# A two-layer decoder trunk on one core: the feed-forward's split weights in a ring of the stage's own pool, and start addresses that differ from pass to pass

## The chip, the core and the metric

The kernel runs on one core of a Trainium2 chip. Its engines work side by side: TensorE (PE) multiplies matrices, VectorE (DVE) and ScalarE (ACT) do elementwise work, GpSimd (POOL) does some of it too, SyncE (SP) issues the transfers. Operands lie in the core's on-chip memory, SBUF, which has 128 partitions; a tile takes the same range of bytes in every partition. Results of TensorE go to PSUM.

The metric is the time of one execution in microseconds of the device, as the median of several runs. Before the change it is 2267.64 us (three runs, 2267.16 to 2267.98).

## What is computed

Two decoder layers on 256 tokens of width 2048, all in float32. The first layer mixes tokens with gated linear attention (GLA), the second with stick-breaking attention; each has a feed-forward stage behind it:

```python
def swiglu(h, w_gate_up, w_down):
    gate, up = jnp.split(h @ w_gate_up, 2, axis=-1)
    return (jax.nn.silu(gate) * up) @ w_down

for layer in range(2):
    a = rmsnorm(h, attn_norm_w[layer])
    h = h + (gla_mixer(a, ...) if layer == 0 else stick_breaking(a, k_shared, v_shared, ...))
    h = h + swiglu(rmsnorm(h, ffn_norm_w[layer]), ffn_w_gate_up[layer], ffn_w_down[layer])
return rmsnorm(h, final_norm_w)
```

`w_gate_up` is 2048 x 11264 and `w_down` 5632 x 2048 in each layer.

## The kernel before

**Split products.** Every large product is made of three matmuls of type float32r: each operand is split into a rounded part and the rest, and `hi*hi`, `hi*lo` and `lo*hi` are added in PSUM. `load_w` (L111) brings weights in pieces of 128 partitions x 1024 values: SP issues the transfer into a `raw` tile (L115), ACT casts it into `hi` (L119), DVE subtracts to get `lo` (L120). `raw` has 4 buffers (pool `wraw`), `hi` and `lo` have 3 each (pool `wsp`), shared by all stages of the program.

**The product.** `gemm_tok` (L123) takes a block of 512 output columns. For each of the K tiles of 128 rows and each of the two token tiles it issues three matmuls (L137): stationary is 128 x 128 of the activations, moving is 128 x 512 of `hi` or `lo`. So each piece of weights feeds 12 matmuls, each with a stationary load of its own.

**Feed-forward.** `ffn` (L247) goes through the 11 blocks of 512 hidden columns in three passes (`PASSES`: 4, 4 and 3 blocks). A pass first makes the hidden blocks: for each, a gate product and an up product over 16 K tiles (192 matmuls), then SiLU, product, and four transposes for each token tile (L266) into `hid_h` and `hid_l`, which are the split stationary operands of the second half. Then `residual_gemm` (L232) multiplies by the pass's rows of `w_down` in four column blocks and adds to `h`. In the last column block of the last pass of layer 1, `gemm_tok_in_turn` (L142) keeps four pieces of weights in a free activation tile.

Matmuls of 512 columns by pass: gate and up 768, 768, 576; down 384, 384, 288. Both layers: 4224 + 2112 = 6336.

**Order.** Instructions of an engine run in the program's order, which a scheduler fixes when the program is built; engines wait for each other by semaphores. A pool's tiles take their place when the pool is opened, and a later pool lies where an earlier one was.

**Addresses.** The allocator starts tiles at multiples of 32 bytes. In the built program every `hi`, `lo`, `xhl` (the split activations), `hid_h` and `hid_l` begins 32 bytes past a multiple of 512, in every buffer; and all slices taken from them step by 512 bytes or a multiple. So each 512-column matmul of the feed-forward begins reading both operands at 32 modulo 512. Tiles of the GLA stage's own pool (`vhl`, `sc_ih`, `sc_il`, `sc_xh`, `sc_xl`, used at L534) begin at 352 modulo 512, which is 96 modulo 128. Those of the attention stage that L607 reads (`fh`, `tri_r`) begin at 32 modulo 512 again.

Of the kernel before, what the change touches and what calls it, by code (L numbers as in the profile page):

```python
# [9 lines left out]
F32R = mybir.dt.float32r  # L10
# [6 lines left out]
P = 128  # L17
D = 2048
S = 256
# [16 lines left out]
DFF = 5632  # L36
LEVELS = (128, 64, 32, 16, 8, 4, 2, 1)
NEG = -1.0e30
PASSES = ((0, 1, 2, 3), (4, 5, 6, 7), (8, 9, 10))


@with_exitstack
def trunk_kernel(
# [20 lines left out]
    v, a, pe, g = nc.vector, nc.scalar, nc.tensor, nc.gpsimd  # L64
# [4 lines left out]
    wsp = ctx.enter_context(tc.tile_pool(name="wsp", bufs=3))  # L69
# [38 lines left out]
        return gains[:, col[key] + k : col[key] + k + 1]  # L108


    def load_w(ap, k0, nk, c0, ncol, dst=None):  # L111
        raw = wraw.tile([P, 1024], F32, name="raw")
        hi, lo = dst or (wsp.tile([P, 1024], F32R, name="hi"), wsp.tile([P, 1024], F32R, name="lo"))
        n = nk * ncol
        nc.sync.dma_start(  # L115
            raw[:, :n].rearrange("p (k c) -> p k c", k=nk),
            ap[k0 * P : (k0 + nk) * P, c0 : c0 + ncol].rearrange("(k p) c -> p k c", p=P),
        )
        a.copy(hi[:, :n], raw[:, :n])  # L119
        v.tensor_tensor(lo[:, :n], raw[:, :n], hi.bitcast(F32)[:, :n], ALU.subtract)  # L120
        return (hi[:, :n].rearrange("p (k c) -> p k c", k=nk), lo[:, :n].rearrange("p (k c) -> p k c", k=nk))

    def gemm_tok(w_ap, kt, lhs, c0, evac, k_row0=0, before=None):  # L123

        acc = [ps_acc.tile([P, NB], F32, name="acc") for _ in range(NT)]
        k0 = 0
        while k0 < kt:
            nk = 1 if before is not None and k0 < 2 else 2
            hi, lo = load_w(w_ap, k_row0 + k0, nk, c0, NB)
            if before is not None:  # L130
                before(k0)
            for j in range(nk):
                k = k0 + j
                for t in range(NT):
                    xh, xl = lhs(k, t)
                    for n, (l, r) in enumerate(((xh, hi), (xh, lo), (xl, hi))):
                        pe.matmul(acc[t], l, r[:, j, :], start=(k == 0 and n == 0), stop=(k == kt - 1 and n == 2))  # L137
            k0 += nk
        for t in range(NT):
            evac(t, acc[t])  # L140

    def gemm_tok_in_turn(w_ap, kt, lhs, c0, evac, k_row0):  # L142

        wh, wl = (w.rearrange("p (n a) s c -> p n (a s c)", n=8)[:, i : i + 4] for w in xt_pair()[2:] for i in (0, 4))
        parts = []
        for i, k0 in enumerate(range(0, kt, 2)):
            parts.append(load_w(w_ap, k_row0 + k0, 2, c0, NB, (wh[:, i, :], wl[:, i, :]) if i < 4 else None))
        for t in range(NT):
            acc = ps_acc.tile([P, NB], F32, name="acc")
            for k in range(kt):  # L150
                xh, xl = lhs(k, t)
                hi, lo = (w[:, k % 2, :] for w in parts[k // 2])
                for n, (l, r) in enumerate(((xh, hi), (xh, lo), (xl, hi))):
                    pe.matmul(acc, l, r, start=(k == 0 and n == 0), stop=(k == kt - 1 and n == 2))  # L154
            evac(t, acc)
# [76 lines left out]
    def residual_gemm(w_ap, kt, lhs, k_row0, after=None, after_tile=None):  # L232

        for nb in range(NCB):
            def evac(t, acc, nb=nb):
                hs = h[:, t, nb * NB : (nb + 1) * NB]
                v.tensor_tensor(hs, acc, hs, ALU.add)  # L237
                if after_tile is not None:
                    after_tile(nb, t)
            if after_tile is not None and nb == NCB - 1:  # L240
                gemm_tok_in_turn(w_ap, kt, lhs, nb * NB, evac, k_row0)
            else:
                gemm_tok(w_ap, kt, lhs, nb * NB, evac, k_row0)
            if after is not None:
                after(nb)

    def ffn(layer, xh, xl, r, **after):  # L247
        w_gu, w_dn = ffn_w_gate_up[layer], ffn_w_down[layer]
        lhs = lambda k, t: (xh[:, k, t * P : (t + 1) * P], xl[:, k, t * P : (t + 1) * P])
        with tc.tile_pool(name=f"ffn{layer}", bufs=2) as fp:  # L250
            for blocks in PASSES:
                hid = []
                for b in blocks:
                    hh = fp.tile([P, 4, S], F32R, name="hid_h", bufs=4)
                    hl = fp.tile([P, 4, S], F32R, name="hid_l", bufs=4)
                    hid.append((hh, hl))
                    sg = [fp.tile([P, NB], F32, name="sg", bufs=4) for _ in range(NT)]

                    def evac_gate(t, acc, sg=sg):
                        a.activation(sg[t], acc, AF.Silu, scale=r[:, t : t + 1])  # L260

                    def evac_up(t, acc, sg=sg, hh=hh, hl=hl):
                        v.scalar_tensor_tensor(sg[t], acc, r[:, t : t + 1], sg[t], ALU.mult, ALU.mult)
                        tp = ps_tr.tile([P, 512], F32, name="tr")
                        for j in range(4):
                            pe.transpose(tp[:, j * P : (j + 1) * P], sg[t][:, j * P : (j + 1) * P], ident)  # L266
                        tv = tp.rearrange("p (j c) -> p j c", j=4)
                        ts = slice(t * P, (t + 1) * P)
                        a.copy(hh[:, :, ts], tv)  # L269
                        v.tensor_tensor(hl[:, :, ts], tv, hh.bitcast(F32)[:, :, ts], ALU.subtract)  # L270

                    gemm_tok(w_gu, KD, lhs, b * NB, evac_gate)
                    gemm_tok(w_gu, KD, lhs, DFF + b * NB, evac_up)

                def hid_lhs(k, t, hid=hid):
                    hh, hl = hid[k // 4]
                    ts = slice(t * P, (t + 1) * P)
                    return hh[:, k % 4, ts], hl[:, k % 4, ts]

                residual_gemm(w_dn, 4 * len(blocks), hid_lhs, blocks[0] * 4, **(after if blocks is PASSES[-1] else {}))  # L280


    w_in = gla_w_in[0]
# [276 lines left out]
    with tc.tile_pool(name="sb", bufs=1) as sp_:  # L560
# [12 lines left out]
        for o in (0, S, ZA, ZA + P):  # L573
            g.affine_select(pen[:, o : o + P], pen[:, o : o + P], [[1, P]], ALU.is_gt, NEG, base=0, channel_multiplier=-1)

# [90 lines left out]
def build(tc, aps):  # L666
    d = dict(zip(_INS, aps))
    d['x'] = d['x'].rearrange("b s d -> (b s) d")
    d['gla_b_gate'] = d['gla_b_gate'].rearrange("l d -> (l d)")
    d['gla_gnorm_w'] = d['gla_gnorm_w'].rearrange("l d -> (l d)")  # L670
    trunk_kernel(tc, *[d[n] for n in _INS], aps[-1].rearrange("b s d -> (b s) d"))
# [20 lines left out]
```

## Time and profile before

| | |
|---|---|
| median of three runs | 2267.64 us |
| the profiled execution's own time | 2267.96 us |
| its span, first to last instruction | 2266.1 us |
| PE busy | 2252.5 us, 10618 matmuls |
| DVE, ACT, POOL busy | 1247.4, 1047.8, 58.0 us |
| transfers | 419.55 MB, 185 GB/s |
| granted TensorE clock | 0.999 of 2.4 GHz over the span |

The profile is one execution. Matmuls overlap in it: the next begins before the one ahead has ended, and ends are modelled, so a matmul's bar is longer than the distance from one start to the next. A busy PE in this profile says that work was always under way, not that the array was at its peak; the distance between starts tells how fast it went.

### The profile page before, as it was taken

To read this page: it belongs to the slowest core of one execution; us is meant where nothing else is said; L and a number is where in the kernel's file an instruction comes from. 1 tells how busy PE (TensorE), PEld (TensorE's weight loads), DVE (VectorE), ACT (ScalarE), POOL (GpSimd) and SP (SyncE) were. 2 spreads that over 40 slices of the span, in tenths; PEclk is the share of its full clock that TensorE was granted. 3 is DMA by queue.
4 is the path that set the end of the run, shared out by engine and by line. 5 is a ranking of instruction groups with operands and counts; after the bars stand their busy time and mean duration, and the time that the engine had idled before them with its cause. 6 is when DMAs were issued, how large, how long until landed. Compare 5 with 4: busy or idle time off the path is not lost.

```text
span 2266.1 us, 27101 instructions
## 1 busy us (share of the span) xinstructions
PE 2252.5 (99%) x10618; PEld 1883.7 (83%) x10618; DVE 1247.4 (55%) x1274; ACT 1047.8 (46%) x1229; POOL 58.0 (3%) x70
## 2 busy tenths in 40 slices
PE   9999999999999999999999999999999999999998
PEld 7888888888888888888888888888888888888886
DVE  6775655554554445445654567655445444554555
ACT  6555455444434443344554446544443344434444
POOL 1100000000000000000000111000000000000000
PEclk9999999999999999999999999999999999999999
DMA  8655555666666666666566654566666666666664
GB/s 233 187 155 149 169 171 189 186 187 191 190 195 188 191 191 193 194 188 192 183 186 191 186 181 145 166 188 186 193 188 193 192 190 190 189 192 192 193 186 158
DMA packets 242782, 419.55 MB, mean 185 GB/s; under 512 B 12962, under 2 KB 64254, under 8 KB 242526
## 3 DMA queue, kind: packets, MB, share of 16 engines
q1 hardware_dynamic: 242478, 416.77, 60.5%
q8 instruction: 83, 1.36, 0.3%
q10 hardware_dynamic: 176, 1.06, 0.1%
q14 instruction: 45, 0.37, 0.0%
HBM read 415.68 MB, written 2.10 MB: 184 GB/s over the span
## 4 chain that ended last, share of the span: by engine, by line
PE 98%; DMA 1%; issue 0%; DVE 0%; ACT 0%; POOLq 0%; POOL 0%; DVEq 0%; SPq 0%; ACTq 0%
PE acc L137 82%; PE acc L169 7%; PE acc L170 4%; PE tr L266 1%; PE px L485 1%; PE tr L196 1%; PE acc L172 0%; DMA raw<-in_gla_w_in_dram 0%; PE acc L154 0%; PE px L534 0%; PE px L589 0%; PE tr L620 0%; DMA h<-in_x_dram 0%; PE px L497 0%; PE tr L621 0%
## 5 line engine op out<-in xcount | busy, mean ns | idle before, releaser
L120 DVE TENSOR_TENSOR lo<-raw,hi 128x1024 fp32r<-128x1024 f32 (+1 forms) x781 | 970.2, 1243 | 918.7 <-ACT hi L119 918.0
L119 ACT CAST hi<-raw 128x1024 fp32r<-128x1024 f32 (+1 forms) x781 | 821.5, 1052 | 1025.7 <-PE acc L137 889.8
L137 PE MATMUL acc<-hi,xhl 128*128 128x512 f32 x4096 | 1273.8, 391 | 0.6 <-ACT xhl L186 0.6
L137 PEld LDWEIGHTS acc<-hi,xhl 128*128 128x128 f32 x4096 | 768.5, 188 | 159.5 <-ACT xhl L186 1.5
L137 PE MATMUL acc<-lo,xhl 128*128 128x512 f32 x2048 | 799.6, 391 | 0.0
L137 PEld LDWEIGHTS acc<-lo,xhl 128*128 128x128 f32 x2048 | 384.8, 188 | 78.9
L137 PE MATMUL acc<-lo,hid_h 128*128 128x512 f32 x680 | 264.9, 390 | 0.0
L137 PE MATMUL acc<-hi,hid_l 128*128 128x512 f32 x680 | 264.6, 389 | 0.0
L169 PE MATMUL acc<-xhl,hi 128*128 128x512 f32 x720 | 250.6, 395 | 0.4 <-ACT hi L119 0.4
L137 PE MATMUL acc<-hi,hid_h 128*128 128x512 f32 x680 | 240.7, 390 | 0.0
L170 PE MATMUL acc<-xhl,lo 128*128 128x256 f32 x768 | 204.7, 281 | 0.0
L169 PEld LDWEIGHTS acc<-xhl,hi 128*128 128x128 f32 x720 | 132.0, 188 | 26.8 <-ACT hi L119 0.8
L170 PEld LDWEIGHTS acc<-xhl,lo 128*128 128x128 f32 x768 | 144.8, 189 | 6.2
L137 PEld LDWEIGHTS acc<-hi,hid_l 128*128 128x128 f32 x680 | 127.7, 188 | 26.4
L137 PEld LDWEIGHTS acc<-hi,hid_h 128*128 128x128 f32 x680 | 127.6, 188 | 26.3
L137 PEld LDWEIGHTS acc<-lo,hid_h 128*128 128x128 f32 x680 | 127.6, 188 | 26.2
L186 ACT ACTIVATE xhl<-tr,gains 128x256 fp32r<-128x256 f32 x96 | 41.0, 470 | 30.7 <-PE tr L196 28.3
L187 DVE SCALAR_TENSOR_TENSOR xhl<-tr,gains,xhl 128x256 fp32r<-128x256 f32 x96 | 42.6, 478 | 17.5 <-ACT xhl L186 17.4
L237 DVE TENSOR_TENSOR h<-acc,h 128x512 f32<-128x512 f32 x64 | 41.2, 682 | 8.5 <-PE acc L154 5.9
L260 ACT ACTIVATE sg<-acc,n_r 128x512 f32<-128x512 f32 x44 | 30.0, 690 | 20.8 <-PE acc L137 20.8
L269 ACT CAST hid_h<-tr 128x512 fp32r<-128x512 f32 x44 | 23.6, 589 | 31.4 <-PE tr L266 31.4
L270 DVE TENSOR_TENSOR hid_l<-tr,hid_h 128x512 fp32r<-128x512 f32 x44 | 28.3, 686 | 17.3 <-ACT hid_h L269 17.3
(177 smaller groups left out, 723.4 us busy)
## 6 DMA issues: line engine op xcount, KB each, us to landing
raw<-in_ffn_w_gate_up_dram SPq DMA_DIRECT2D x352, 512.0 KB, 3.8
raw<-in_ffn_w_down_dram SPq DMA_DIRECT2D x176, 512.0 KB, 3.7
raw<-in_gla_w_in_dram SPq DMA_DIRECT2D x97, 512.0 KB, 3.8
raw<-in_sb_w_kv_dram SPq DMA_DIRECT2D x64, 512.0 KB, 3.9
raw<-in_gla_w_out_dram SPq DMA_DIRECT2D x32, 512.0 KB, 3.7
raw<-in_sb_w_q_dram SPq DMA_DIRECT2D x32, 512.0 KB, 3.6
raw<-in_sb_w_out_dram SPq DMA_DIRECT2D x32, 512.0 KB, 3.8
h<-in_x_dram SPq DMA_DIRECT2D x8, 256.0 KB, 6.4
```

The source lines that it names most:

```text
L119: a.copy(hi[:, :n], raw[:, :n])
L120: v.tensor_tensor(lo[:, :n], raw[:, :n], hi.bitcast(F32)[:, :n], ALU.subtract)
L137: pe.matmul(acc[t], l, r[:, j, :], start=(k == 0 and n == 0), stop=(k == kt - 1 and n == 2))
L169: pe.matmul(acc[c], hi[:, j, cs], both, start=first, stop=False)
L170: pe.matmul(acc[c][:, :S], lo[:, j, cs], xhl[:, k0 + j, 0, :], start=False, stop=False)
L186: a.mul(dst_h, src, scale)
L187: v.scalar_tensor_tensor(dst_l, src, scale, dst_h.bitcast(F32), ALU.mult, ALU.subtract)
L196: pe.transpose(tp[:, o : o + P], src(t)[:, j * P : (j + 1) * P], ident)
L237: v.tensor_tensor(hs, acc, hs, ALU.add)
L260: a.activation(sg[t], acc, AF.Silu, scale=r[:, t : t + 1])
L269: a.copy(hh[:, :, ts], tv)
L270: v.tensor_tensor(hl[:, :, ts], tv, hh.bitcast(F32)[:, :, ts], ALU.subtract)
```

## The change

The feed-forward no longer uses the shared ring for its split weights. While `ffn` runs, `load_w` takes them from the stage's pool, as `fhi` and `flo`, three buffers each. These tiles, and `hid_h` and `hid_l`, are 64 values longer than what is used of them, and the part in use begins at an offset that the table `PLACES` gives for each pass: one for the weights of the gate and up products, one for those of the down product, one for the hidden tiles. The arithmetic, the transfers, the matmuls and their number stay.

```diff
+PAD = 64
+
+PLACES = (((4, 8, 8), (8, 24, 24), (16, 56, 56)), ((24, 0, 4), (32, 0, 32), (48, 0, 2)))
 PASSES = ((0, 1, 2, 3), (4, 5, 6, 7), (8, 9, 10))
...
+    ring = lambda name: wsp.tile([P, 1024], F32R, name=name)
+
+    def shifted(pool, shape, o, name, bufs):
+
+        n = shape[0] * shape[1]
+        return pool.tile([P, n + PAD], F32R, name=name, bufs=bufs)[:, o : o + n].rearrange("p (a b) -> p a b", a=shape[0])
+
     def load_w(ap, k0, nk, c0, ncol, dst=None):
         raw = wraw.tile([P, 1024], F32, name="raw")
-        hi, lo = dst or (wsp.tile([P, 1024], F32R, name="hi"), wsp.tile([P, 1024], F32R, name="lo"))
+        hi, lo = dst or (ring("hi"), ring("lo"))
...
     def ffn(layer, xh, xl, r, **after):
+        nonlocal ring
+        outer = ring
...
         with tc.tile_pool(name=f"ffn{layer}", bufs=2) as fp:
-            for blocks in PASSES:
+            place = 0
+            ring = lambda name: shifted(fp, (1, 1024), place, "f" + name, 3)[:, 0, :]
+            for n_pass, blocks in enumerate(PASSES):
                 hid = []
+                place, place_down, place_hid = PLACES[layer][n_pass]
                 for b in blocks:
-                    hh = fp.tile([P, 4, S], F32R, name="hid_h", bufs=4)
-                    hl = fp.tile([P, 4, S], F32R, name="hid_l", bufs=4)
+                    hh = shifted(fp, (4, S), place_hid, "hid_h", 4)
+                    hl = shifted(fp, (4, S), place_hid, "hid_l", 4)
...
+                place = place_down
                 residual_gemm(w_dn, 4 * len(blocks), hid_lhs, blocks[0] * 4, **(after if blocks is PASSES[-1] else {}))
+        ring = outer
```

With the places of the built program the operands of the 512-column matmuls then begin, in bytes modulo 128 (before: 32 everywhere):

| layer, pass | gate and up: moving, stationary | matmuls | down: moving, stationary | matmuls |
|---|---|---|---|---|
| 0, first | 48, 32 | 768 | 64, 64 | 384 |
| 0, second | 64, 32 | 768 | 0, 0 | 384 |
| 0, third | 96, 32 | 576 | 0, 0 | 288 |
| 1, first | 0, 32 | 768 | 32, 48 | 384 |
| 1, second | 32, 32 | 768 | 32, 32 | 384 |
| 1, third | 96, 32 | 576 | 32, 40 | 288 |

The padded tiles are 4352 bytes long, so neighbouring buffers, and `hi` and `lo` of one piece, differ by 256 modulo 512, where they were equal.

Two rings also let the scheduler move instructions where a feed-forward stage begins; elsewhere the order on all engines is the same. On ACT, at the entry of layer 0's stage, `hi` and `fhi` being the cast weights of the output projection before it and of the feed-forward, and `xhl` the activations that the last norm block writes. Before:

```order
L119 CAST hi<-raw 128x1024 x6
L204 ACTIVATE junk,ss<-h 128x512 x2
L119 CAST hi<-raw 128x1024
L186 ACTIVATE xhl<-tr,gains 128x256 x2
L119 CAST hi<-raw 128x1024
```

After:

```order
L129 CAST hi<-raw 128x1024
L129 CAST fhi<-raw 128x1024
L129 CAST hi<-raw 128x1024
L129 CAST fhi<-raw 128x1024
L129 CAST hi<-raw 128x1024
L129 CAST fhi<-raw 128x1024
L214 ACTIVATE junk,ss<-h 128x512
L129 CAST fhi<-raw 128x1024
L214 ACTIVATE junk,ss<-h 128x512
L129 CAST fhi<-raw 128x1024
L196 ACTIVATE xhl<-tr,gains 128x256 x4
```

The first casts of the feed-forward now stand between the last ones of the projection, and two of them ahead of or within the sums of squares.

On PE, at the same entry, before, with the last eight transposes of `h` (L196) and weights of both products under the name `hi`:

```order
L137 MATMUL acc<-lo,xhl 128x512
L137 MATMUL acc<-hi,xhl 128x512
L196 MATMUL tr<-ident,h 128x128 x2
L137 MATMUL acc<-hi,xhl 128x512
L196 MATMUL tr<-ident,h 128x128 x6
L137 MATMUL acc<-lo,xhl 128x512
```

After, where the feed-forward's first matmuls begin:

```order
L147 MATMUL acc<-lo,xhl 128x512
L147 MATMUL acc<-hi,xhl 128x512
L147 MATMUL acc<-fhi,xhl 128x512 x2
L147 MATMUL acc<-hi,xhl 128x512 x2
L147 MATMUL acc<-flo,xhl 128x512
L147 MATMUL acc<-fhi,xhl 128x512
L147 MATMUL acc<-flo,xhl 128x512
```

The feed-forward's first matmul stands 24 matmuls earlier, among the last of the projection, and the eight transposes 8 later than before. The entry of layer 1's stage has the same two shifts.

## Rows read from the trace of the kernel before

**Rows 1.** The page: its first line, and PE's busy time.

```profile
span 2266.1 us, 27101 instructions
PE 2252.5 (99%) x10618; PEld 1883.7 (83%) x10618; DVE 1247.4 (55%) x1274; ACT 1047.8 (46%) x1229; POOL 58.0 (3%) x70
```

**Rows 2.** The page's chain that ended last, by engine.

```profile
PE 98%; DMA 1%; issue 0%; DVE 0%; ACT 0%; POOLq 0%; POOL 0%; DVEq 0%; SPq 0%; ACTq 0%
```

**Rows 3.** Stages: length, busy of PE, PEld, DVE, ACT, POOL, clock, DMA, GB/s.

```profile
677.00:853.00 176.00, 176.00 (x790) 146.02 (x789) 86.67 (x78) 75.72 (x78) 0.00 (x0) 1.00 0.64 190
1971.00:2058.00 87.00, 87.00 (x390) 72.12 (x389) 44.47 (x42) 34.84 (x34) 0.00 (x0) 1.00 0.61 190
```

**Rows 4.** Line L137 alone in two stretches: PE (matmuls), PEld, clock, DMA, GB/s.

```profile
595.00:720.00 125.00, 125.00 (x553) 103.52 (x552) 1.00 0.63 192
860.00:985.00 125.00, 125.00 (x554) 103.48 (x553) 1.00 0.63 193
```

**Rows 5.** PE's groups by form: busy us, mean ns of one, idle before.

```profile
L137 PE MATMUL acc<-hi,hid_l 128*128 128x512 f32 x680 | 264.6, 389 | 0.0
L169 PE MATMUL acc<-xhl,hi 128*128 128x512 f32 x720 | 250.6, 395 | 0.4 <-ACT hi L119 0.4
L589 PE MATMUL px<-qp,kk 128*128 128x256 f32 x32 | 9.5, 379 | 0.0
```

**Rows 6.** PE's timeline, GLA stage, 247 to 251 us: start, length, instruction.

```profile
247.64 0.39 PE L137 MATMUL acc<-lo,xhl 128*128 128x512 f32 x1
...
248.55 0.39 PE L534 MATMUL px<-vhl,sc_ih 128*128 128x512 f32 x1
248.78 0.39 PE L534 MATMUL px<-vhl,sc_xh 128*128 128x512 f32 x1
249.00 0.63 PE L137 MATMUL acc<-hi,xhl 128*128 128x512 f32 x2
...
251.09 0.39 PE L137 MATMUL acc<-lo,xhl 128*128 128x512 f32 x1
```

**Rows 7.** PE's timeline, attention stage, 1437 to 1438 us.

```profile
1436.95 0.39 PE L137 MATMUL acc<-hi,xhl 128*128 128x512 f32 x1
...
1438.08 0.39 PE L607 MATMUL tr<-fh,tri_r 128*128 128x512 f32 x1
1438.31 0.28 PE L609 MATMUL tr<-fh,tri_r 128*128 128x256 f32 x1
```

**Rows 8.** PE's timeline behind the transposes of a hidden block.

```profile
725.82 0.48 PE L137 MATMUL acc<-hi,xhl 128*128 128x512 f32 x1
726.14 0.40 PE L137 MATMUL acc<-lo,xhl 128*128 128x512 f32 x1
726.37 0.62 PE L137 MATMUL acc<-hi,xhl 128*128 128x512 f32 x2
```

**Rows 9.** Who waited for whom: us in total, times, longest.

```profile
DVE lo L120 <- ACT hi L119: 918.0, 730, 5.0
ACT hi L119 <- PE acc L137: 889.8, 541, 3.7
```

**Rows 10.** Entry of layer 0's feed-forward: last `og` transposes, first weight transfers, PE.

```profile
L196 PE MATMUL tr<-ident,og x32: 270/272/273, 259.3 to 334.6; 128*128 128x128 f32 x32
397.37 5.85 SPq L115 DMA_DIRECT2D raw<-in_ffn_w_gate_up_dram  x3
405.49 0.84 PE L137 MATMUL acc<-hi,xhl 128*128 128x512 f32 x3
415.92 0.38 PE L196 MATMUL tr<-ident,h 128*128 128x128 f32 x2
```

**Rows 11.** The page: landing time of feed-forward weights, and the two splitting instructions.

```profile
raw<-in_ffn_w_gate_up_dram SPq DMA_DIRECT2D x352, 512.0 KB, 3.8
L120 DVE TENSOR_TENSOR lo<-raw,hi 128x1024 fp32r<-128x1024 f32 (+1 forms) x781 | 970.2, 1243 | 918.7 <-ACT hi L119 918.0
L119 ACT CAST hi<-raw 128x1024 fp32r<-128x1024 f32 (+1 forms) x781 | 821.5, 1052 | 1025.7 <-PE acc L137 889.8
```

## The prediction

> **What bounds the kernel.** I read the page's busy times first, then the chain, then the stages, then single starts. PE is busy for 2252.5 of 2266.1 us [rows 1], and the chain that ended last is 98% PE [rows 2]. In the feed-forward PE is busy all the time, at the full granted clock (1.00, the 2.4 GHz level), while DVE and ACT are busy for half of it or less [rows 3]. So nothing feeds PE too late there; only the number of matmuls and the distance from one start to the next count.
>
> That distance is the quantity to look at. In 125 us of a down product 553 or 554 matmuls are under way [rows 4]; with one bar of 0.39 us more, 125.39 us / 553 or 554 is 226.3 to 226.7 ns. A bar is 389 ns [rows 5], so a bar is the distance and some 162 ns. 512 columns at one each tick of 2.4 GHz are 213.3 ns; each matmul thus costs 13.3 ns over its columns. For 6336 matmuls of the feed-forward that is 84 us. This is all that addresses could touch; the rest is columns.
>
> Does it depend on addresses? Two places of the trace speak to it.
> - A matmul that reads tiles at 352 modulo 512 among such that read at 32 upsets the rhythm [rows 6]. From 247.64 to 248.55 us there are four starts (0.91 us, 227 ns each, within the rounding of the view). From the first L534 at 248.55 to L137 at 251.09 there are eleven (the rows left out hold the seven that aren't shown): 2.54 us, 231 ns each.
> - L607 changes the tiles, the PSUM buffer and the waits too, but its operands begin at 32. From 1436.95 to 1438.31 there are six starts in 1.36 us, 227 ns each, L607's own among them [rows 7]. It upsets nothing.
>
> So I take it that a start address can matter for the distance, by some ns, and that a stream left alone finds back to 226.7: behind the transposes of a hidden block the distances are 320, 230 and some 230 ns, and then 226.7 [rows 8]. What no row shows is a long stream whose operands begin at unlike places, or all at another place than 32. That is the unknown of this change.
>
> **The change part by part.**
>
> *The ring.* 528 pieces of weights (352 and 176) are still brought, cast and subtracted, with 4 `raw` buffers and 3 of each split tile. The cast is 1052 ns and the subtraction 1243 ns [rows 11] per piece, which PE uses for 12 x 226.7 = 2720 ns. ACT's casts wait 889.8 us for PE to free a buffer [rows 9], so PE is the one waited for, and a cast that took half as long again would still be hidden. Cost 0; the same for offsets that might slow ACT or DVE.
>
> *The entries.* Two rings let the first three pieces be split before the projection's last ones are used up. PE isn't idle there, so nothing is gained. It could lose: the first feed-forward matmul now stands 24 matmuls earlier, where PE was at about 405.7 us, within the three matmuls that begin from 405.49 on [rows 10]. Its piece was sent for at 397.37 [rows 10]; with 3.8 us to landing [rows 11] and 1.05 + 1.24 us for the split it is there at 403.5 us. That leaves 2.2 us, if ACT takes it at once; ACT's order has it between two casts of the projection, one of which may wait for PE, 3.7 us at the longest [rows 9]. So 0 to 1.5 us at each of the two entries; I take 0, since 2.2 us of slack is nearer to the usual wait (889.8 us in 541 times, 1.6 us each). The new tiles lie where GLA's tiles were, whose last readers are the `og` transposes at 334.6 us, 63 us before the first transfer [rows 10], so no release is waited for. The eight transposes that move stay eight: 0.
>
> *The addresses.* The sum is (matmuls of a pass) x (new distance - 226.7 ns). The bounds of the new distance, from the nearest rows:
> - Below: L589 is a plain float32 matmul of 256 columns with the same stationary load. Its bar is 379 ns [rows 5], so its distance is some 217 ns, or 520 ticks: two a column and 3.7 ns over. It reads its moving tile half as fast, so it is far from our case, but it is the least overhead that a row shows. At 217 ns a matmul gains 9.7.
> - Above: 231 ns while upset [rows 6], and 395 - 162 = 233 ns for L169 [rows 5], which has matmuls of 512 and 256 columns in turn and all starts at 32. So +4.2 to +6.3 ns.
> - Nearest is 226.7 itself: the same instructions, in all of 57 long stretches of the trace whatever tiles they read (xhl, hid, `gemm_tok_in_turn`'s too), come back to it within ten matmuls of every upset.
>
> I take 226.7, since a value to which the stream returns from any state looks like a property of the two streams, not of one lucky start. The kicks at the twelve changes of place are at most like those behind transposes: some 10 matmuls x 4 ns, 0.5 us in all, 0 to 1.
>
> Sum: 2267.96 us of the profiled execution + 0 + 0 + 0.5 = 2268.4, and as the median was 0.3 lower, 2268.
>
> The Trainium skill, "SBUF — State Buffer", section "Who interferes with whom", gives PE two SBUF read ports, one for the moving operand and one for stationary loads, and says that PE never waits on anyone. By that rule addresses change nothing, and the sum would be the 2268 above; the upset at L534 is a row that doesn't fit it well. The skill's "TensorE: Matmul & The Clock Gate", section "Back-to-back issue gap", gives an isolated matmul N/2.4 + 2.5 ns, 216 for 512 columns. By that, if all 13.3 ns above the columns were a matter of addresses, 6336 x 10.9 = 69 us would be the most to gain (an estimate from that page).
>
> **The rivals.**
>
> *B, slower: the streams don't settle.* Before, both operands of each feed-forward matmul begin at the same place modulo 512. After, they differ modulo 128 in seven of the twelve halves of passes: gate and up of layer 0 (768, 768, 576) and of the first and third pass of layer 1 (768, 576), and down of layer 1's first and third pass (384, 288), 4128 matmuls. If what settles the rhythm is that both streams start at like places, these stay at 231: 4128 x 4.2 ns = +17 us, 2285. It decides as soon as a quarter of them do (1070 x 4.2 = 4.5 us). For it: the upset at L534 is of this sort, and the mean while upset is above the settled value, so that whatever replaces the settled state is likelier worse than better. Against: the upset heals within some ten matmuls, and there the operands were alike with each other and only unlike the ones ahead. If 256 matter too (neighbouring buffers and `hi` against `lo` differ by 256 modulo 512), all 6336 are touched: +27 us, 2295; if a third of the 4128 are, +6, 2274.
>
> *C, faster: like places at a better boundary.* At 32 modulo 64 each run of 2048 bytes touches one block of 64 more than from 0. Moving operands begin at 0 modulo 64 in the down products of layer 0 (1056) and in gate and up of two passes (1536), 2592 matmuls. At the lower bound they gain 9.7 ns: -25 us, 2243; at half of it -13, 2255. For it: 13.3 ns on a stream that nothing stops asks for a cause, and L589 shows most of it gone when the moving tile is read half as fast, which points to the reading. Against: no row of the trace has a moving start at 0 modulo 64 in this type, and the skill's two ports speak of no blocks.
>
> *D: the change doesn't do what it says.* The offsets are in the built program's addresses, so this can only be that an offset has no effect, which is the forecast.
>
> **How the numbers follow.** Less than 0.2% (4.5 us, about what a measurement of this kernel can tell from none) counts as the same: 2263 to 2272. The forecast has 0.42, with a range of its own of 2265 to 2271. B has 0.40: the trace shows that addresses disturb, and its settled state is at the low end of what disturbed matmuls show; some 0.08 of it lies above 2287 (the 256 matter, or 233 ns), and the rest between 2272 and 2287. C has 0.18, most of it at 2252 to 2263, some 0.07 below. Cutting 0.07 and 0.08 leaves 2252 to 2287. Faster 0.18, same 0.42, slower 0.40.
>
> **What would show it.** In the profile after, the count of L147 matmuls in windows within each half of a pass tells its distance; compare with 226.7. The forecast says that all twelve are within 0.5 ns. B says that the seven named are at 228 to 233 and the five others at 226.7; C that the down products of layer 0 are below 226. PE's first matmuls at the two entries show a wait if ACT's new order costs something: PE's idle time at about 405 and 1523 us would be above zero. I am wrong if the distance in some half of a pass moves by more than 2 ns, and wrong in the ring if PE idles in the feed-forward.

## The result: 28 us slower

The changed kernel takes 2295.41 us (median of four runs, 2294.53 to 2296.6) where the kernel before took 2267.4 beside it. The ratio is 1.0123, with a 95% interval of 1.0111 to 1.0135. The forecast was 2268 with a range of 2252 to 2287: it named the wrong case, and the range ended 8 us too low.

The page of the changed kernel, its first line, its engines and the chain that ended last (before: [rows 1, 2]):

```profile
span 2292.7 us, 27095 instructions
PE 2279.0 (99%) x10618; PEld 1884.0 (82%) x10618; DVE 1247.8 (54%) x1274; ACT 1044.1 (46%) x1229; POOL 57.7 (3%) x70
PE 99%; issue 0%; DMA 0%; DVE 0%; ACT 0%; SPq 0%; POOLq 0%; POOL 0%; DVEq 0%; ACTq 0%
```

The span grew by 26.6 us and PE's busy time by 26.5. Everything else stayed, the number of matmuls and the time of the stationary loads (PEld, 1883.7 and 1884.0 us) included. The kernel was bound by PE and is bound by PE; PE got slower with the same instructions. All waits of PE, from the view of waits (who waited for whom, us in total, times, longest):

```profile
PE tr L107 <- POOL mf L347: 3.8, 1, 3.8
PE acc L147 <- ACT xhl L196: 1.3, 1, 1.3
PE tr L206 <- DMA h<-in_x_dram: 0.2, 1, 0.2
```

These belong to the program's start, the last of them ahead of the matmul at 7.83 us. So neither the feed-forward nor its entries let PE wait. The first matmuls with the new ring, from PE's timeline at the entry of layer 0's stage (start, length, instruction; before: [rows 10]):

```profile
404.63 0.39 PE L147 MATMUL acc<-hi,xhl 128*128 128x512 f32 x1
404.86 0.62 PE L147 MATMUL acc<-fhi,xhl 128*128 128x512 f32 x2
405.32 0.63 PE L147 MATMUL acc<-hi,xhl 128*128 128x512 f32 x2
405.79 0.40 PE L147 MATMUL acc<-flo,xhl 128*128 128x512 f32 x1
```

They follow each other at 230 to 235 ns with no gap. Now the feed-forward. The stage of [rows 3], all engines, and PE's groups of two of its products (busy us, mean ns of one, idle; before, bars of the same kinds were 389 to 391 ns, [rows 5] for one):

```profile
677.00:853.00 176.00, 176.00 (x769) 141.83 (x768) 85.00 (x76) 73.23 (x76) 0.00 (x0) 1.00 0.63 186
```

```profile
L147 PE MATMUL acc<-fhi,xhl 128*128 128x512 f32 x2816 | 888.4, 395 | 0.0
L147 PE MATMUL acc<-fhi,hid_l 128*128 128x512 f32 x680 | 265.7, 391 | 0.0
```

The stretch from 677 to 853 us is as busy as before and at the same granted clock, but holds 769 matmuls instead of 790. The busy share says nothing of this; the count does.

One window lies in each of the twelve halves of passes, line L147 alone (columns: length, PE's busy time and matmuls, PEld, clock, DMA share, GB/s). Odd lines are gate and up, even ones down:

```profile
406.00:590.00 184.00, 181.70 (x781) 146.26 (x780) 1.00 0.62 186
592.00:679.00 87.00, 86.37 (x381) 71.21 (x380) 1.00 0.60 190
681.00:861.00 180.00, 178.11 (x762) 142.28 (x761) 1.00 0.63 186
863.00:949.00 86.00, 85.37 (x377) 70.40 (x376) 1.00 0.61 192
951.00:1082.00 131.00, 129.74 (x566) 105.90 (x565) 1.00 0.63 189
1085.00:1118.00 33.00, 31.96 (x139) 25.67 (x138) 1.00 0.56 186
1534.00:1720.00 186.00, 183.70 (x784) 146.63 (x783) 1.00 0.61 184
1722.00:1808.00 86.00, 85.37 (x377) 70.34 (x376) 1.00 0.61 190
1811.00:1990.00 179.00, 177.11 (x759) 142.21 (x758) 1.00 0.62 186
1992.00:2080.00 88.00, 87.37 (x377) 70.57 (x376) 1.00 0.60 187
2082.00:2216.00 134.00, 132.74 (x568) 105.83 (x568) 1.00 0.63 186
2218.00:2283.00 65.00, 49.38 (x212) 39.36 (x210) 1.00 0.52 167
```

Line L137 of the kernel before, in three of the same windows:

```profile
406.00:590.00 184.00, 181.70 (x798) 149.10 (x797) 1.00 0.63 189
592.00:679.00 87.00, 86.37 (x381) 71.24 (x380) 1.00 0.62 191
681.00:861.00 180.00, 177.48 (x780) 145.77 (x780) 1.00 0.64 191
```

PE's busy time over the count is within about 1 ns of the distance from start to start: 181.70 / 798 = 227.7 ns before in the first window, 181.70 / 781 = 232.7 after. The down product from 592 to 679 us has 381 matmuls in both. For finer numbers I worked out the mean distance between successive starts for each half, from all starts of the half that are under 260 ns apart (so without the step behind transposes). D is the start of the moving operand less that of the stationary one, modulo 256 bytes:

| layer, pass | gate and up: moving, stationary modulo 256 | D | ns | down: moving, stationary | D | ns |
|---|---|---|---|---|---|---|
| 0, first | 48, 32 | 16 | 231.64 | 64, 64 | 0 | 226.85 |
| 0, second | 64, 32 | 32 | 233.33 | 128, 128 | 0 | 226.88 |
| 0, third | 96, 32 | 64 | 228.95 | 0, 0 | 0 | 227.28 |
| 1, first | 128, 32 | 96 | 233.34 | 32, 48 | 240 | 227.05 |
| 1, second | 160, 32 | 128 | 232.87 | 32, 160 | 128 | 232.34 |
| 1, third | 224, 32 | 192 | 233.36 | 32, 40 | 248 | 230.65 |

Before, the settled distance is 226.67 ns everywhere. Summed from start to start, L137's matmuls with `xhl` as the stationary operand (projections, gate and up) went from 1402.8 to 1426.2 us, the down products from 479.8 to 483.3; 23.4 + 3.5 = 26.9 us, which is the whole change of the span (the matmuls of layer 1's last column block, L154 before and L164 after, are counted with the down products). Every other group of PE has the time that it had before, within 0.6 us.

### The profile page after: what moved, and what is told of

The parts are those of the page before. It is cut to its first block, busy times and chain, and to the rows that moved or that the text cites. A ratio compares the mean times of both kernels' runs of the same rounds, so it can differ in the third digit from the quotient of the medians.

```text
span 2292.7 us, 27095 instructions
## 1 busy us (share of the span) xinstructions
PE 2279.0 (99%) x10618; PEld 1884.0 (82%) x10618; DVE 1247.8 (54%) x1274; ACT 1044.1 (46%) x1229; POOL 57.7 (3%) x70
## 4 chain that ended last, share of the span: by engine, by line
PE 99%; issue 0%; DMA 0%; DVE 0%; ACT 0%; SPq 0%; POOLq 0%; POOL 0%; DVEq 0%; ACTq 0%
PE acc L147 82%; PE acc L179 7%; PE acc L180 4%; PE tr L281 1%; PE px L502 1%; PE tr L206 1%; PE acc L182 0%; PE acc L164 0%; PE px L551 0%; PE px L606 0%; PE tr L637 0%; DMA raw<-in_gla_w_in_dram 0%; PE acc L368 0%; PE px L514 0%; PE px L607 0%
## 5 line engine op out<-in xcount | busy, mean ns | idle before, releaser
L130 DVE TENSOR_TENSOR flo<-raw,fhi 128x1024 fp32r<-128x1024 f32 x524 | 642.0, 1225 | 706.5 <-ACT fhi L129 706.4
L129 ACT CAST fhi<-raw 128x1024 fp32r<-128x1024 f32 x524 | 549.0, 1048 | 782.6 <-PE acc L147 758.7
L147 PE MATMUL acc<-fhi,xhl 128*128 128x512 f32 x2816 | 888.4, 395 | 0.0
L147 PEld LDWEIGHTS acc<-fhi,xhl 128*128 128x128 f32 x2816 | 528.6, 188 | 124.3
L147 PE MATMUL acc<-flo,xhl 128*128 128x512 f32 x1408 | 554.7, 394 | 0.0
L130 DVE TENSOR_TENSOR lo<-raw,hi 128x1024 fp32r<-128x1024 f32 (+1 forms) x257 | 328.3, 1279 | 230.1 <-ACT hi L129 229.8
L147 PE MATMUL acc<-hi,xhl 128*128 128x512 f32 x1280 | 402.1, 393 | 1.3 <-ACT xhl L196 1.3
L129 ACT CAST hi<-raw 128x1024 fp32r<-128x1024 f32 (+1 forms) x257 | 269.0, 1047 | 258.4 <-PE acc L147 138.2
L147 PEld LDWEIGHTS acc<-flo,xhl 128*128 128x128 f32 x1408 | 264.3, 188 | 62.5
L147 PEld LDWEIGHTS acc<-hi,xhl 128*128 128x128 f32 x1280 | 240.1, 188 | 51.0 <-ACT xhl L196 2.1
L147 PE MATMUL acc<-flo,hid_h 128*128 128x512 f32 x680 | 265.9, 391 | 0.0
L147 PE MATMUL acc<-fhi,hid_l 128*128 128x512 f32 x680 | 265.7, 391 | 0.0
L147 PE MATMUL acc<-lo,xhl 128*128 128x512 f32 x640 | 251.7, 394 | 0.0
L147 PE MATMUL acc<-fhi,hid_h 128*128 128x512 f32 x680 | 241.7, 392 | 0.0
L147 PEld LDWEIGHTS acc<-fhi,hid_l 128*128 128x128 f32 x680 | 127.8, 188 | 27.4
L147 PEld LDWEIGHTS acc<-flo,hid_h 128*128 128x128 f32 x680 | 127.8, 188 | 27.2
L147 PEld LDWEIGHTS acc<-fhi,hid_h 128*128 128x128 f32 x680 | 127.8, 188 | 27.2
L147 PEld LDWEIGHTS acc<-lo,xhl 128*128 128x128 f32 x640 | 120.5, 188 | 24.7
```

## Experiments

### Ring and pads without offsets

```diff
-PLACES = (((4, 8, 8), (8, 24, 24), (16, 56, 56)), ((24, 0, 4), (32, 0, 32), (48, 0, 2)))
+PLACES = (((0, 0, 0), (0, 0, 0), (0, 0, 0)), ((0, 0, 0), (0, 0, 0), (0, 0, 0)))
```

> The changed kernel with every offset at zero: own ring, padded tiles and the moved instructions at the stage entries stay; each moving and stationary operand begins at 32 modulo 256 again (neighbouring buffers still differ by 256). Theory 'difference' (what counts is the start of the moving operand minus that of the stationary one, modulo 256 bytes): all distances 226.7 ns, 2267 to 2270 us. Rival 'ring' (the ring, the pads, the 256 between hi and lo or the entries cost): 2280 to 2296 us, with distances above 228 ns or PE idle at the entries. Rival 'place' (any operand that doesn't begin at 32 costs) says 2267 to 2270 too.

Measured: 2267.58 us against 2267.9, ratio 0.9999 (0.9989 to 1.0009). All twelve halves are at 226.7 to 227.1 ns. L147 in two windows:

```profile
690.00:850.00 160.00, 158.11 (x696) 130.12 (x695) 1.00 0.64 190
1811.00:1960.00 149.00, 147.11 (x648) 121.00 (x647) 1.00 0.65 190
```

158.11 / 696 is 227.2 ns. So the ring, the new order at the entries, the longer tiles, and buffers that differ by 256 modulo 512 cost nothing together. All 28 us are the offsets'.

### All operands moved, but alike

The activations that gate and up read are padded and moved too, so that moving and stationary operands begin alike again, at 96 modulo 256 in layer 0 and at 192 in layer 1 (only 48 matmuls of the block that keeps its weights in a free tile stay unlike).

```diff
+PLACES = (((16, 16, 16), (16, 16, 16), (16, 16, 16)), ((40, 40, 40), (40, 40, 40), (40, 40, 40)))
...
-    def xt_pair():
-        t = xt.tile([P, KD, 2, S], F32R, name="xhl")
+    def xt_pair(o=0):
+        t = xt.tile([P, KD * 2 * S + PAD], F32R, name="xhl")
+        t = t[:, o : o + KD * 2 * S].rearrange("p (k s c) -> p k s c", k=KD, s=2)
...
-    fh, fl, _ = xt_pair()
+    fh, fl, _ = xt_pair(16)
...
-    fh, fl, _ = xt_pair()
+    fh, fl, _ = xt_pair(40)
```

> Both operands moved together: in layer 0 activations, weights and hidden tiles all begin 64 bytes later (96 modulo 256), in layer 1 160 bytes later (192 modulo 256), in all passes. Only 48 matmuls of the last column block, whose weights lie in an activation tile, are unlike. Theory 'difference': distances of 226.7 to 227 ns everywhere, 2267 to 2272 us. Rival 'place': gate and up products at 229 ns or more, 2280 to 2296 us.

Measured: 2268.06 us in one run (before: 2267.9); all halves at 226.7 to 227.5 ns. L147 again:

```profile
690.00:850.00 160.00, 158.11 (x695) 130.05 (x695) 1.00 0.65 191
1811.00:1960.00 149.00, 147.11 (x647) 120.86 (x647) 1.00 0.65 191
```

One matmul fewer than without any offset, in each window. So a start is not good or bad by itself; where both operands start alike the distance is the old one, at 32, at 96, at 192, and in the changed kernel's own down products at 64, 128 and 0. In each of these it settles at 226.67 ns; means above that come from the first ten to twenty starts behind transposes or a change of place, which lie between 224 and 236 ns.

The split tiles are also written at the shifted places, by ACT and DVE, while PE reads. The changed kernel's trace speaks against these writes as the cause: in its eight halves with a loss, the mean distance while ACT is busy and while it isn't differs by 0.2 ns at most (231.5 and 231.7 in the first gate half, 233.2 and 233.2 in the second), and with DVE by 0.4 at most.

### Gates alone, downs alone

Offsets as in the change for one half of each pass, zero for the other:

```diff
+PLACES = (((0, 8, 8), (0, 24, 24), (0, 56, 56)), ((0, 0, 4), (0, 0, 32), (0, 0, 2)))
```

> The changed kernel with the gate and up offsets back at zero, all else as changed. Theory 'difference, modulo 256': the gate and up products are at 226.7 ns again, which takes back 23 of the 27 us; the down products stay as they were (layer 1's second 232.3 and third 230.7 ns, the others 226.9 to 227.3), +3 to +4 us: 2270 to 2272 us. If the loss came from elsewhere than these distances: 2280 or more.

```diff
+PLACES = (((4, 0, 0), (8, 0, 0), (16, 0, 0)), ((24, 0, 0), (32, 0, 0), (48, 0, 0)))
```

> The other part alone: gate and up offsets as changed, down and hidden offsets at zero. Theory 'difference, modulo 256': the gate distances are those of the changed kernel (231.6, 233.3, 229.0, 233.3, 232.9, 233.4 ns), the down products at 226.7 to 227: 2267.5 + 23.5 = 2290 to 2292 us, and with the run that has only the down offsets the two losses add up to that of the change within 3 us. If they don't add: below 2288 or above 2295.

Measured: with the gates at zero, 2273.5 us against 2267.3, ratio 1.0027 (1.0018 to 1.0037). With the downs at zero, 2291.22 against 2267.44, ratio 1.0105 (1.0088 to 1.0122), and its gates are at 231.64, 233.32, 228.95, 233.39, 232.86 and 233.34 ns, as in the changed kernel. L147 of the kernel with the downs at zero, in a gate half of layer 0 (158.11 / 676 is 233.9 ns):

```profile
690.00:850.00 160.00, 158.11 (x676) 126.18 (x676) 1.00 0.63 185
```

The two losses are 6.2 and 23.8 us, together 30.0, and the change lost 28.0. The second kernel came as expected; the first missed its 2270 to 2272 us by 1.5.

The 2 us over have a place. L147 of the kernel with the gates at zero, in a gate half of layer 0 and in the first two down products of layer 1:

```profile
690.00:850.00 160.00, 158.11 (x696) 130.05 (x695) 1.00 0.64 190
1710.00:1795.00 85.00, 84.37 (x363) 68.05 (x362) 1.00 0.60 186
1977.00:2063.00 86.00, 85.37 (x369) 68.92 (x368) 1.00 0.60 188
```

The second line is the product whose operands start at 32 and 48. Its mean distance is 232.98 ns here and 227.05 in the changed kernel, with the same starts: 384 x 5.93 ns = 2.3 us. Only what ran ahead of it differs. That is followed up below.

### Other differences

Two kernels with other differences in each half, with the stationary operand at 32. They look for a difference that is better than none, and for a rule.

```diff
+PLACES = (((60, 63, 0), (2, 61, 0), (12, 58, 0)), ((20, 56, 0), (28, 52, 0), (36, 44, 0)))
```

> One difference for each half of a pass, activations and hidden tiles at 32, weights shifted by (in bytes) gate and up 240, 8, 48, 80, 112, 144; down 252, 244, 232, 224, 208, 176. Theory 'difference': 240 (that is -16) gives 227.0 in gate and up as it gave in a down product of the changed kernel; 8 and 48 lie between 227 and 233, the others at 229 to 233.5; no difference is below 226.7 by more than 0.5 ns. Rival 'a better place exists': some difference is settled at 225 ns or below. In all 2280 to 2300 us by the first, less by the second.

```diff
+PLACES = (((63, 1, 0), (1, 2, 0), (40, 4, 0)), ((44, 12, 0), (56, 40, 0), (52, 10, 0)))
```

> As the scan before, gate and up 252, 4, 160, 176, 224, 208; down 4, 8, 16, 48, 160, 40. Theory 'difference': the same difference gives the same distance within 0.5 ns in a gate and a down product, so that 252, 4, 160, 176, 208, 224 and 8, 48 repeat what their partners show in either scan, and 16 in a down product gives 231.6 as it did in a gate product of the changed kernel. Rival 'products differ' (other stationary tiles, other buffers): partners differ by more than 1 ns.

Measured: 2305.73 and 2308.42 us, one run each. The first was expected at 2280 to 2300, with 227.0 ns for a gate product at D = 240 and no more than 233.5 elsewhere; it measured 235.8 there, and 239.7 at D = 244. L147 of the first in its second gate half (D = 8):

```profile
690.00:850.00 160.00, 158.11 (x677) 128.03 (x677) 1.00 0.63 184
```

And of the second in the first three halves (D = 252, 4, 4):

```profile
407.00:589.00 182.00, 179.70 (x785) 146.56 (x784) 1.00 0.64 189
591.00:681.00 90.00, 89.37 (x378) 70.95 (x377) 1.00 0.59 184
683.00:865.00 182.00, 180.10 (x760) 142.67 (x759) 1.00 0.62 183
```

The mean distances by D, with those of the changed kernel and of other kernels' gates added (ns; one number is gate and up unless it says down, two are gate and up, then down):

| D | ns | D | ns | D | ns | D | ns |
|---|---|---|---|---|---|---|---|
| 0 | 226.7 to 227.5 | 64 | 229.0 | 136 | 233.3 | 208 | 234.7, 234.7 |
| 4 | 236.6, 236.7 | 72 | 235.5 | 144 | 233.3 | 216 | 234.2 |
| 8 | 233.1, 232.8 | 80 | 231.1 | 152 | 233.4 | 224 | 233.3, 233.3 |
| 16 | 231.6, 231.7 | 88 | 232.8 | 160 | 234.3, 234.3 | 232 | down: 233.9 |
| 24 | 233.4 | 96 | 233.3 | 168 | 233.3 | 240 | 235.8; down: see below |
| 32 | 233.3 | 104 | 232.3 | 176 | 232.2, 231.2 | 244 | down: 239.7 |
| 40 | down: 233.9 | 112 | 228.8 | 184 | 232.2 | 248 | down: 230.7 |
| 48 | 232.1, 230.2 | 120 | 234.7 | 192 | 233.4 | 252 | 227.8, 227.9 |
| 56 | 232.3 | 128 | 232.9, 232.3 | 200 | 232.8 |  |  |

No difference that was tried is better than none. The loss doesn't grow with the difference: 4 bytes one way cost 10 ns and 4 bytes the other way 1. It isn't a period of 128 either: 128 apart costs 6 ns. Gate and down products agree to 0.3 ns for D = 4, 8, 16, 160, 208, 224 and 252, differ by 0.5 for 128, and by 1 to 2 ns for 48 and 176. In nearly all of the table's unlike rows the stationary operand begins at 32, so that a difference comes with one start of the moving operand. Whether other starts with the same difference give the same distance was tried at 128, with two pairs of starts (232.9 and 232.3 ns), and at -16 (below), where they don't.

### Which stationary tile: the matmul's own or the next

While a matmul streams, the load of the next one runs beside it (in the kernel before a load of 0.19 us starts at 999.91 us together with a matmul of 0.39; the next matmul starts at 1000.13). Two theories: what counts is the start of the moving operand against its own stationary tile, or against the next. In the down products `hi` and `lo` of weights and hidden tiles get places of their own; in the first kernel `lo` weights and `hid_l` move together, in the second the `lo` weights alone, by 32, 64, 96, 128, 192 and 240 bytes.

```diff
+            ring = lambda name: shifted(fp, (1, 1024), place[name], "f" + name, 3)[:, 0, :]
...
+                    hh = shifted(fp, (4, S), hid_at["hi"], "hid_h", 4)
+                    hl = shifted(fp, (4, S), hid_at["lo"], "hid_l", 4)
```

> Down products: lo weights and the low stationary tile hid_l are shifted together by 32, 64, 96, 128, 192, 240 bytes (one value for each half), hi and hid_h stay. The matmuls of a K tile run hi on hid_h, lo on hid_h, hi on hid_l, and while one streams, the stationary of the one behind it is loaded. Theory 'next' (the moving operand meets the load of the NEXT stationary): hi meets hid_h, lo meets hid_l, hi meets the next hid_h, all alike, so 226.7 to 227.5 ns in all six. Rival 'own' (a matmul's moving against its own stationary): two of three are unlike, 229 ns or more as in the scans. Gate and up: only lo is shifted by the same values, one of three is unlike in either theory: 227 to 234 ns; below 226 would show that a better state exists.

> Down products: lo weights alone shifted by 32, 64, 96, 128, 192, 240 bytes, the stationary tiles stay; against the run that shifts hid_l with lo. One of three matmuls is unlike in either theory ('next': lo meets hid_l; 'own': lo on hid_h): 227 to 234 ns. If 'next' holds, shifting hid_l too repairs this in the other run; if 'own' holds, the other run is slower than this one, since two of three are unlike there. Gate and up: differences of 72, 104, 136, 168, 200, 216 bytes, 227 to 236 ns; 225 or below would be a better place.

Measured (2295.39 and 2306.75 us, one run each; in the gates the first moves `lo` alone, by the same six values, and the second moves both, for other differences of the table), in ns:

| `lo` moved by | 32 | 64 | 96 | 128 | 192 | 240 |
|---|---|---|---|---|---|---|
| down, `lo` and `hid_l` | 232.0 | 230.6 | 229.6 | 230.6 | 231.7 | 231.4 |
| down, `lo` alone | 231.9 | 232.7 | 231.7 | 230.8 | 230.6 | 229.3 |
| gate and up, `lo` alone | 232.1 | 232.4 | 232.1 | 230.6 | 231.0 | 229.1 |

The products' line (L154 in these kernels) in the first down half, of the first kernel and of the second (whose window begins 1 us ahead of the half):

```profile
594.00:681.00 87.00, 86.37 (x373) 69.69 (x372) 1.00 0.60 187
595.00:684.00 89.00, 88.37 (x382) 71.33 (x381) 1.00 0.60 188
```

The two rows with `lo` alone agree within 0.4 ns, though the products, the stationary tiles and the kernels differ.

The theory of the next tile expected 226.7 to 227.5 in the first row and falls. The theory of the matmul's own tile has two of three matmuls unlike in the first row and one of three in the second, and would have the second row clearly lower; it isn't. So it isn't shown either. One unlike matmul in three is enough to lose 2 to 6 ns on the mean of all three. Who pays differs: in the gate products with `lo` moved by 240, the step that follows a `lo` matmul is 233.2 ns and the two others 227.0 and 227.1; with `lo` moved by 32 they are 233.9, 231.0 and 231.2, so all three pay.

### 16 bytes below: two settled values

The half that measured 227.05 and 232.98 ns has D = 240, the moving operand 16 bytes below the stationary one. One kernel with this difference at six places (the gates have other differences of the table), and one with the changed kernel's 32 and 48 in all six down products, and all gates alike:

```diff
+     ({'hi': 6, 'lo': 6}, {'hi': 60, 'lo': 60}, {'hi': 0, 'lo': 0}),
+     ({'hi': 14, 'lo': 14}, {'hi': 0, 'lo': 0}, {'hi': 4, 'lo': 4}),
+     ({'hi': 22, 'lo': 22}, {'hi': 4, 'lo': 4}, {'hi': 8, 'lo': 8}),
+     ({'hi': 30, 'lo': 30}, {'hi': 8, 'lo': 8}, {'hi': 12, 'lo': 12}),
+     ({'hi': 38, 'lo': 38}, {'hi': 16, 'lo': 16}, {'hi': 20, 'lo': 20}),
+     ({'hi': 46, 'lo': 46}, {'hi': 28, 'lo': 28}, {'hi': 32, 'lo': 32})
```

> Down products: one difference, -16 bytes, at six places (moving, stationary modulo 256: 16,32; 32,48; 48,64; 64,80; 96,112; 144,160), since it gave 227.0 ns at 32,48 and 235.8 in a gate product at 16,32. Theory 'difference alone': all six the same. Rival 'difference and alignment': 16,32 and 48,64 are alike and slow (about 236), 32,48, 64,80 and 96,112 (moving at a multiple of 32) about 227. Gate and up: differences of 24, 56, 88, 120, 152, 184 bytes, 227 to 236 ns; one at 225 or below would be a better place than the kernel before has.

```diff
+PLACES = (((0, 0, 4),) * 3, ((0, 0, 4),) * 3)
```

> Gate and up at zero; in all six down products the weights begin at 32 and the hidden tiles at 48 modulo 256, the difference of -16 bytes at which one down product was at 227.05 ns in the changed kernel and at 232.98 ns when only the gate offsets were taken back. Theory 'two settled states' (which one is entered hangs on the moment the stream starts): a mixture, some halves at 227 and some at 233, not all the same, and nothing between. Rival 'what the gates left behind' (a gate product at zero ahead of it decides): all six at 233, 2267.5 + 6.2 us for 1056 + 1056 matmuls, 2280 at most.

Measured, first kernel (2306.75 us): moving starts at 16, 48 and 144 give 236.6, 236.4 and 236.2 ns; at 32, 64 and 96 they give 233.3, 227.05 and 227.04. Its L154 in the down products of layer 0's first two passes and layer 1's first two (16, 32, 64, 96):

```profile
595.00:684.00 89.00, 88.37 (x374) 70.89 (x373) 1.00 0.59 183
868.00:955.00 87.00, 86.37 (x371) 69.67 (x370) 1.00 0.60 187
1735.00:1821.00 86.00, 85.37 (x377) 70.36 (x376) 1.00 0.61 190
2005.00:2091.00 86.00, 85.37 (x377) 70.32 (x376) 1.00 0.62 190
```

Second kernel (2280.07 us): 232.98, 232.98, 230.04, 232.98, 232.98 and 232.78 ns. The third is a mixture in time. PE's timeline there, at a change of state and at one back:

```profile
1080.21 0.39 PE L147 MATMUL acc<-fhi,hid_l 128*128 128x512 f32 x1
...
1082.47 0.39 PE L147 MATMUL acc<-fhi,hid_h 128*128 128x512 f32 x1
...
1083.16 1.03 PE L281 MATMUL tr<-ident,sg 128*128 128x128 f32 x8
1083.95 0.48 PE L147 MATMUL acc<-fhi,hid_h 128*128 128x512 f32 x1
1084.27 0.40 PE L147 MATMUL acc<-flo,hid_h 128*128 128x512 f32 x1
...
1085.67 0.39 PE L147 MATMUL acc<-flo,hid_h 128*128 128x512 f32 x1
...
1118.97 0.82 PE L206 MATMUL tr<-ident,h 128*128 128x128 f32 x6
1119.54 0.47 PE L147 MATMUL acc<-flo,hid_h 128*128 128x512 f32 x1
1119.86 0.39 PE L147 MATMUL acc<-fhi,hid_l 128*128 128x512 f32 x1
...
1121.44 0.39 PE L147 MATMUL acc<-fhi,hid_h 128*128 128x512 f32 x1
```

From 1080.21 to 1082.47 there are ten distances, 2.26 us: 226 ns. From 1084.27 to 1085.67 there are six, 1.40 us: 233 ns. From 1119.86 to 1121.44 there are seven, 1.58 us: 226 ns. Same tiles, same starts modulo 256, and each time eight or six transposes ahead. So with the moving operand 16 bytes below (at multiples of 32), two rhythms hold themselves up, and they change behind transposes. In single starts of the halves with this difference (moving at a multiple of 32), the step behind the transposes was 312 ns three times, and 227 followed each time; 314 or 315 seven times, and 233 followed; 317 four times, and each followed twice. That the moment of entry chooses the rhythm is an idea from these fourteen steps, and wasn't tested. The first kernel's halves at 64 and 96 begin at 233, and are at 227 from their first transposes on. In the second kernel it's the other way round: each half begins at 227 (226.65 to 226.70 over its first 21 starts), and the first transposes bring 233. So the rival by which the product ahead decides had five of the six means, but by luck: the gates at zero leave 227 behind them, and what follows is set later. And the place within 32 matters here as well: with the moving start at 16 modulo 32 the same difference gives 236 ns, so 'difference alone' falls.

### The changed kernel a second time

> The changed kernel once more, for a second profile. If each half of a pass has one distance, all twelve repeat within 0.3 ns. If there are two settled states for some differences, layer 1's first down product (-16 bytes, 227.05 before) may be at 233, with the total up by 2.3 us; the gate products repeat.

Measured: 2294.4 us in one run. The means of all twelve halves are within 0.03 ns of those of the first profile, the half at 227.05 too. So the changed kernel's distances aren't chance of one execution: the same program fell into the same states in both.

## Why the prediction was wrong

**The step that failed** is the address term: "I take 226.7, since a value to which the stream returns from any state looks like a property of the two streams". It is a property of two streams *that start alike*. All of the 57 stretches that I counted as evidence had their operands at the same place modulo 256; they were one case seen 57 times, not 57 cases. The one row that showed something else, the upset at L534 [rows 6], had the sign right, and I let its healing outweigh it, though I had written that it heals among operands that are alike with each other. What the runs show in place of 226.7 is 229.0 to 233.4 ns in the six gate halves, and 230.7 and 232.3 in two down halves, 26.9 us in all. That the upset's 231 ns lies among these values is luck. L534's own two operands begin alike (352 modulo 512) and only its neighbours begin elsewhere, so the row shows a change of place and not a settled rhythm of unlike streams; behind transposes, too, the matmuls have operands that are alike, and their first distances are 230 ns [rows 8].

**Rival B had the mechanism**, with two mistakes in its working. Its price was 4.2 ns; the unlike halves measured 2.3 to 6.7 more than 226.67, but for layer 1's first down product with 0.4, and 3.5 us / 2112 = 1.7 ns as a mean over all down matmuls, 23.4 us / 4224 = 5.5 ns over gates and ups. And it counted likeness modulo 128: 4128 matmuls. The second pass of layer 1, 768 and 384 matmuls at a difference of 128, was put among the undisturbed and ran at 232.9 and 232.3 ns: 768 x 6.2 + 384 x 5.7 = 7.0 us more than B allowed. B's own line on 256 named that case at 2295, the time measured, but as a case of all 6336 matmuls in which neighbouring buffers count as well. They don't (first experiment: 226.7 ns); the 2295 came out of a wrong count and a low price.

**The range** ended at 2287, with 0.08 of B above it. The upper row that I had cited myself, 233 ns [rows 5], times the unlike matmuls would have been 4128 x 6.3 = 26 us, 2294. The range should have reached to the rows of its own bounds. That 2294 comes close to the measured time is luck too: L169's starts are all alike, so its 233 ns doesn't come from unlike starts. It has matmuls of 512 and 256 columns in turn; like starts gave 226.67 only in streams of 512 columns each. And the 13.3 ns over the columns, "all that addresses could touch", bounded only a gain: at D = 244 a matmul costs 26 ns over its columns.

**Rival C** falls: with the moving start at 0 modulo 64 and both alike, the down products of layer 0 ran at 226.85 to 227.28 ns, not below 226; with the moving start at 0 modulo 64 and unlike, 233.3. The 216 ns that the Trainium skill's "TensorE: Matmul & The Clock Gate", section "Back-to-back issue gap", gives for an isolated matmul of 512 columns were reached by no half of any kernel; the lowest mean is 226.7.

**Right** were the ring, the entries and the longer tiles, at 0 each: ACT and DVE have the same busy times within 4 us, PE waits nowhere but at the program's start, and the kernel without offsets takes 0.9999 of the time before. The twelve kicks at 0.5 us weren't measured apart from the rest.

The rule that the prediction weighed, the Trainium skill's "SBUF — State Buffer", section "Who interferes with whom" (two read ports of PE, which never waits on anyone), doesn't agree with the runs if it is read as speaking of PE's two streams: with the same instructions, the same clock and no wait in the profile, matmuls begin 226.7 ns apart or 233, as the starts of their operands are alike or not. As a sentence on other engines no run here speaks against it.

**What stays open.** Which pair collides. Successive moving streams with each other can't be the whole of it: in the scans `hi` and `lo` move together, so that moving operands are alike among themselves, and the distances are 228 to 240 ns all the same. Nor can the next stationary tile (first row of that experiment's table). The matmul's own stationary tile isn't excluded, but the same rows don't bear it out, and more than one pair may count. Nor is it known where in the chip it happens, why 4 bytes above cost 10 ns and 4 below cost 1, or why differences of 48 and 176 aren't worth the same in both products. No kernel that ran beats the one before: operands alike, at the 226.67 ns it has, are the best found.

## What to carry to other kernels

When PE is the bound, the mean distance between starts is to be read beside the busy share: here 28 us were lost with PE at 99% in both kernels and no wait of PE in the feed-forward of either. In streams of float32r matmuls of 512 columns with a stationary load each, let moving and stationary tiles begin alike modulo 256 bytes, and look at the addresses after any change of pools, pads or tile sizes; offsets of 8 to 224 bytes, such as can come in by themselves, cost 1.2% here. And a row that repeats is one piece of evidence, however often, as long as what is to be changed was the same each time.

## What was not expected of the hardware

- The settled distance of like streams of 512 columns, 226.67 ns, holds at every common start tried (0, 32, 64, 96, 128, 192 modulo 256), and unlike streams have distances of their own, with means of 228 to 240 ns (227 in one rhythm at -16 bytes); those of the changed kernel repeated to 0.03 ns in a second execution.
- A difference of 128 bytes is unlike (232.9 ns), one of 256 is like (226.7 ns).
- At a difference of -16 bytes two rhythms exist, 227.05 and 232.98 ns, within one product and with the same tiles.
- One unlike moving operand in three slows the mean of all three by 2 to 6 ns (229.1 to 232.7 against 226.7).
